# A decoder trunk on one core: a beginning with direct fp32 products, and three of four gate blocks as split fp32r products

## The chip, the cores and the metric

The kernel runs on one core of a Trainium2 chip. The metric is the device time of one execution in microseconds. The engines have these short names in the profile: PE (TensorE, matrix products), PEld (its weight loads), DVE (VectorE), ACT (ScalarE), POOL (GpSimd) and SP (SyncE, which issues most of the loads). Every engine has a queue of its own and works through it in order; they wait for each other by semaphores.

## The reference

The input is 256 tokens of 1024 features in float32. Layer 0 mixes tokens by a recurrent block, layer 1 by sparse attention; each is followed by an MLP with squared ReLU. Before each part stands an RMS norm, after it a residual addition. The change lies in the recurrent block:

```python
def _rglru_mixer(h, w_in, conv_w, conv_b, w_a, b_a, w_x, b_x, lam, w_out):
    proj = h @ w_in
    y = jax.nn.gelu(proj[..., :D_RNN], approximate=True)
    xb = _causal_depthwise_conv(proj[..., D_RNN:], conv_w, conv_b)
    xr = xb.reshape(B, S, RG_BLOCKS, RG_BLOCK_W)            # 4 blocks of 256
    r = jax.nn.sigmoid(jnp.einsum('bsnc,ncd->bsnd', xr, w_a).reshape(B, S, D_RNN) + b_a)
    i = jax.nn.sigmoid(jnp.einsum('bsnc,ncd->bsnd', xr, w_x).reshape(B, S, D_RNN) + b_x)
    log_a = -RG_C * r * jax.nn.softplus(-lam)
    a = jnp.exp(log_a)
    u = jnp.sqrt(-jnp.expm1(2.0 * log_a)) * (i * xb)
    _, hs = lax.associative_scan(_lru_combine, (a, u), axis=1)
    return (hs * y) @ w_out
```

## The kernel before

Features lie on the 128 partitions, tokens in the free dimension: a chunk is 128 features of 256 tokens, and there are eight (k = 0 to 7). Weights come in pieces of 128 by 1024 floats (512 KB), each holding the eight 128 by 128 blocks that give one chunk of output.

**Split products.** A float32 product is made of three fp32r products: weights and inputs are each split into a high part (a copy cast to fp32r) and a low part (the difference), and `mm3` adds high times high, high times low and low times high in PSUM (lines 344 to 346 in the profile). A piece is loaded by SP into a ring of raw tiles, cast to `whi` by ACT or DVE, and its `wlo` is made by DVE (lines 360 and 353). Pieces named in `AWAY` go another way: POOL issues a load that casts on its way into `whi` (line 384), ACT or DVE writes the negative into `wlo` (lines 356 and 357), and POOL issues the same load again, which adds into `wlo` (line 399).

**Direct products.** Gate blocks that are not in `GSPLIT`, which are blocks 0 and 1, keep raw float32 weights in tiles `gw`, and TensorE multiplies them as float32 (line 787).

**The order of the work.** The recurrent section is a list of tasks, each with engines, an assumed duration, keys that it reads and writes, and a wished time. `Plan.emit` makes an order from these in Python, before the kernel is built, with a seed (`SEEDS`), and emits every task into its engine's queue in that order. Assumed durations and lags of loads thus set the order, not the time. The order of the pieces is `RG_ORDER`: c0 to c7 are the input products with the conv behind them, y0 to y7 those of the gelu branch, g0 to g3 the gate blocks. Ring slots are given out by position in this order.

**The beginning.** SP loads the input x in four parts and the first three pieces (`NFINE`) in two halves each, in the order of `FIRST` ("x0" is chunks 0 and 1, "10" the first half of piece 1). Meanwhile TensorE runs 18 products of zeros (`WARM`, line 653), and eight more after the second chunk of piece 0. For every chunk ACT makes the high part `hh` of x times the norm's weight and DVE the low part `hl` (lines 660 and 662); for every quarter of the first three pieces the high and low parts are made separately. The norm's row scale `rs` is applied only to the product (lines 748 and 823), so that products begin before it is known.

**Behind it.** `conv` scales a product, runs the four taps on DVE and splits the result `xb` for the blocks in `GSPLIT`; `gate` makes the two gates by tanh (line 790), then the decay `r` and `t` (lines 797 and 799), which need `sp` and `nsp`. Those come from a softplus of the parameter lambda, computed on tiles of 128 by 8 as a polynomial (lines 693 to 708). `scan` takes the square root and runs the recurrence on DVE chunk by chunk (line 818), `product` multiplies by the gelu branch and splits the result (lines 830, 831, 360, 353), and the output projection follows.

Of the kernel before, what the change touches and what calls it, by code (L numbers as in the profile page):

```python
# [41 lines left out]
RG_ORDER = [(x[0], int(x[1])) for x in "c0 c1 c2 c3 c4 c5 c6 c7 y0 g0 g1 g2 y1 g3 y2 y3 y4 y5 y6 y7".split()]  # L42
# [11 lines left out]
GSPLIT = (2, 3)  # L54
AWAY = [("in", 1), ("in", 2), ("in", 4), ("in", 6)]
# [171 lines left out]
def trunk_kernel(ctx: ExitStack, tc: tile.TileContext, x_in, vec_in, const_in, w2_in, wts, out):  # L227
# [139 lines left out]
    class Section:  # L367
# [21 lines left out]
        def split(self, i, t, lead):  # L389
            t -= lead + AHEAD * away[i]  # L390
            self.load(i, t)
            n = piece_cols(order[i][0])
            hi, lo, rw = hi_t[i % NSPL], lo_t[i % NSPL], raw_of(i)
            rk = raw_key(i)
            if away[i] and i >= self.seen["split"]:
                hk, lk = ("hi", i % NSPL), ("lo", i % NSPL)
                self.add([("act", 0.95, 0.0), ("dve", 0.63, HPEN)], minus(lo[:, :n], hi[:, :n].bitcast(F32)), r=[hk], w=[lk], t=t)
                self.add("sp", ADD[0], lambda e: None, r=[hk], w=[("slot", -i), lk], t=t, lag=0.0)
                self.add("pool", ADD[1], lambda e: e.dma_start(lo[:, :n], source(i), accum_op=OP.add), r=[("slot", -i)], w=[lk], t=t, lag=ADD[2])
                self.seen["split"] = self.seen["lo"] = i + 1  # L400
            if i >= self.seen["split"]:
# [33 lines left out]
        def proj(self, name, idx, b, t, step, xs=None, xk=None, wide=False):  # L435
            wh, wl, wk = self.weight(name, idx, t)
            z = self.bank((name, idx), b, (lambda x: x) if wide else zcols)
            xs, xk = xs or [(hhw[:, k], hlw[:, k]) for k in range(KC)], xk or hkey
            for i in range(0, 4, self.join):
# [9 lines left out]
                self.add("pe", 0.68 * self.join, run, r=wk + list(xk[ks.start:ks.stop]), w=[("ps", b)], t=t + i * step)  # L449
# [161 lines left out]
    with ExitStack() as ph:  # L611
# [12 lines left out]
        def first_x(k):  # L624
            a, b = KC * (k > 0) + k * S, KC + (k + 2) * S
            src = x_in[P * a:P * b].rearrange("(p n) -> p n", p=P)
            first_load(xgt[:, a:b], src, [("xt", k), ("xt", k + 1)] + ["vec0"] * (k == 0), 0.66, 3.6 if k else 2.0)

        def first_w(i, q):
            o = offs[i] + P * q * 256  # L630
            src = wts[o:o + P * 512].rearrange("(p n) -> p n", p=P)
            first_load(raw_t[i][:, q * 256:q * 256 + 512], src, [("raw0", i, q), ("raw0", i, q + 1)], 0.66, 3.6 if q or i else 2.1)
        sec.plan.busy.update(pool=0.5, act=0.4, pe=4.4)
# [22 lines left out]
        x2 = rg.tile([P, KC, S], F32, name="x2")  # L656
        for k in range(KC):
            g = gm0[:, k:k + 1]
            t = 0.6 * k - 3
            add("act", 0.4, lambda e, k=k, g=g: e.activation(hh[:, k], xt[:, k], AF.Identity, scale=g),  # L660
# [28 lines left out]
        NT = 9  # L689
        cj = [1.0 / (2 * j + 1) for j in range(NT + 1)]  # L690
        V = ["vec"]
        small = lambda fn, r=(), w=(), eng="pool", t=8.0: add(eng, 0.45 if eng == "pool" else 0.1, fn, r=list(r), w=list(w), t=t)
# [4 lines left out]
        small(lambda e: e.tensor_scalar(s8, e8, 2.0, None, op0=OP.add), ["e8"], ["s8"], "dve")  # L697
# [4 lines left out]
        for j in range(NT - 1, 0, -1):  # L702
            small(lambda e, j=j: e.scalar_tensor_tensor(ac, ac, cj[j], s2, op0=OP.add, op1=OP.mult), ["s2"], ["ac"], "dve")
        small(lambda e: e.scalar_tensor_tensor(ac, ac, cj[0], s8, op0=OP.add, op1=OP.mult), ["s8"], ["ac"], "dve")
        small(lambda e: e.tensor_scalar(ac, ac, 2.0, None, op0=OP.mult), [], ["ac"])
        small(lambda e: e.tensor_tensor(sp, ac, nsp, op=OP.add), ["ac", "nsp"], ["sp"])
# [23 lines left out]
        def conv(m, t):  # L730
            b = nextbank()
            if m < NFINE:
                wh, wl, _ = sec.weight("in", 8 + m, t)
                z, zk = sec.bank(("in", 8 + m), b, zcols), ("ps", b)
                for k in range(KC):
                    def run(e, k=k):
                        w = slice(k * P, (k + 1) * P)
                        mm3(z(), wh[:, w], wl[:, w], hhw[:, k], hlw[:, k], k == 0, k == KC - 1)
                        if m == 0 and k == 1:
                            keep_warm(8)  # L740
                    add("pe", 0.323 + 0.9 * (m == 0 and k == 1), run, r=[("hi0", m, k // 2), ("lo0", m, k // 2), ("hi", m), ("lo", m), hkey[k]],
# [12 lines left out]
            if m // 2 not in GSPLIT:  # L754
# [12 lines left out]
        def gate(b, t):  # L767
# [27 lines left out]
            for m in ms:  # L795
# [10 lines left out]
                r=keys("r", m), w=keys("i", m), t=t + 3)  # L806

        def scan(m, t):
# [4 lines left out]
            for m in ms:  # L813
                if m % 2 == 0:
                    ip, tp = pair(i_b, m), pair(t_b, m)
                    add("dve", 0.6, lambda e, ip=ip, tp=tp: e.tensor_tensor(ip, ip, tp, op=OP.mult), r=keys("t", m),
                        w=keys("i", m), t=t)
                add("dve", 0.59, lambda e, m=m: e.tensor_tensor_scan(t_t[m], r_t[m], i_t[m], 0.0, op0=OP.mult, op1=OP.add),
                    r=[("r", m), ("i", m)], w=[("t", m)], t=t + 0.5)
# [852 lines left out]
```

## Time and profile before

| | |
|---|---|
| median of 3 runs | 549.14 us (549.08 to 549.91) |
| profiled execution | 548.89 us, of which the span 547.1 us |
| PE busy | 539.4 us, 99% of the span |
| PEld busy | 502.8 us |
| DVE busy | 444.2 us, 81% |
| ACT busy | 363.9 us, 67% |
| POOL busy | 28.0 us, 5% |
| TensorE clock granted, mean | 0.998 |
| loads and stores | 105.63 MB, mean 193 GB/s |

A row of a timeline gives the start, the duration (the first start to the last end where several alike are merged), the engine, the line, the operation with its output and inputs, and how often; in brackets stands the idle time before it and what ended that. A row of a group ends with the busy time in us, the mean in ns and the idle time before. The shares of busy time are means over stages with different limits, so the recurrent section, about the first 70 us, is read by itself.

### The profile page before, as it was taken

Reading aid. Unit: us, or ns where it says so; the run is one execution under the profiler, and the core shown is the slowest. Engines: PE = TensorE matmul, PEld = TensorE weight load, DVE = VectorE, ACT = ScalarE, POOL = GpSimd, SP = SyncE. Lnnn points to the kernel's source line nnn. Section 1 sums busy time; section 2 is a strip of 40 time slices with the busy share of each in tenths; the row PEclk is TensorE's granted clock in tenths of the full one; section 3 lists DMA queues with packets and bytes.
Section 4 is the critical chain, followed back from the end, with each engine's and each line's share of the span. In section 5 each row is a group of like instructions: output and inputs, shape, how many; then the busy total and the mean of one; then the engine's idle time right before and its main releaser. Section 6 shows DMA issues by size and latency. Waiting matters only on the chain.

```text
span 547.1 us, 10280 instructions
## 1 busy us (share of the span) xinstructions
PE 539.4 (99%) x3766; PEld 502.8 (92%) x3766; DVE 444.2 (81%) x969; ACT 363.9 (67%) x739; POOL 28.0 (5%) x50
## 2 busy tenths in 40 slices
PE   9999999999999999999999999999999999999995
PEld 9999999999998889999999999999999998888895
DVE  7999999797777456898939999989797778977945
ACT  7799666697877334346747999966787876433422
POOL 1131000000000000173000000000000000000000
PEclk9999999999999999999999999999999999999999
DMA  8977665486667764458765431353487666765502
GB/s 317 403 199 234 186 220 183 166 281 209 211 198 230 244 211 148 160 168 265 258 193 189 133 112 55 122 192 104 169 262 202 199 213 206 262 209 180 153 0 78
DMA packets 34690, 105.63 MB, mean 193 GB/s; under 512 B 3920, under 2 KB 9296, under 8 KB 34640
## 3 DMA queue, kind: packets, MB, share of 16 engines
q1 hardware_dynamic: 32432, 100.26, 56.1%
q0 software_dynamic: 1152, 4.19, 3.3%
q8 instruction: 30, 0.49, 0.4%
q10 hardware_dynamic: 1056, 0.52, 0.3%
q14 instruction: 20, 0.16, 0.1%
HBM read 101.32 MB, written 1.05 MB: 187 GB/s over the span
## 4 chain that ended last, share of the span: by engine, by line
PE 85%; DVE 8%; DMA 3%; ACT 2%; issue 1%; DVEq 0%; ACTq 0%; SPq 0%
PE bank L349 24%; PE bank L350 12%; PE bank L604 8%; PE bank L605 8%; PE bank L603 8%; PE bank L346 5%; PE bank L344 5%; PE bank L345 5%; PE bank L1332 3%; DVE wlo L353 2%; DMA raw<-in_dram 2%; PE bank L1313 2%; DVE xb L752 2%; PE bank L1259 1%; PE bank L1260 1%; PE bank L1166 1%
## 5 line engine op out<-in xcount | busy, mean ns | idle before, releaser
L349 PE MATMUL bank<-hhl,whi 128*128 128x512 f32 x512 | 167.9, 382 | 0.0
L288 ACT CAST whi<-raw 128x1024 fp32r<-128x1024 f32 x116 | 121.0, 1049 | 60.4 <-PE bank L605 57.8
L297 DVE TENSOR_TENSOR wlo<-raw,whi 128x1024 fp32r<-128x1024 f32 x115 | 141.9, 1236 | 23.3 <-ACT whi L288 22.8
L350 PE MATMUL bank<-hhl,wlo 128*128 128x256 f32 x512 | 139.6, 273 | 0.0
L349 PEld LDWEIGHTS bank<-hhl,whi 128*128 128x128 f32 x512 | 96.9, 189 | 13.4
L350 PEld LDWEIGHTS bank<-hhl,wlo 128*128 128x128 f32 x512 | 98.5, 192 | 0.0
L353 DVE TENSOR_TENSOR wlo<-raw,whi 128x1024 fp32r<-128x1024 f32 (+2 forms) x70 | 74.4, 1088 | 2.5 <-ACT whi L360 2.5
L603 PE MATMUL bank<-whi,uhl 128*128 128x512 f32 (+1 forms) x206 | 75.3, 366 | 0.0
L605 PE MATMUL bank<-whi,uhl 128*128 128x512 f32 (+1 forms) x206 | 75.2, 365 | 0.0
L604 PE MATMUL bank<-wlo,uhl 128*128 128x512 f32 (+1 forms) x206 | 75.2, 365 | 0.0
L344 PE MATMUL bank<-hhl,whi 128*128 128x256 f32 x256 | 70.7, 276 | 0.2 <-DVE tt L1090 0.2
L346 PE MATMUL bank<-hhl,wlo 128*128 128x256 f32 x256 | 70.6, 276 | 0.0
L345 PE MATMUL bank<-hhl,whi 128*128 128x256 f32 x256 | 70.5, 275 | 0.0
L360 ACT CAST whi<-raw 128x1024 fp32r<-128x1024 f32 (+2 forms) x60 | 58.8, 998 | 11.5 <-PE bank L345 6.1
L879 DVE CUSTOM_DVE_ANT_0 t<-bank,s 128x256 f32<-128x256 f32 x64 | 27.1, 423 | 34.4 <-ACT s L877 34.2
L344 PEld LDWEIGHTS bank<-hhl,whi 128*128 128x128 f32 x256 | 49.2, 192 | 0.2 <-PE bank L1120 0.2
L346 PEld LDWEIGHTS bank<-hhl,wlo 128*128 128x128 f32 x256 | 49.2, 192 | 0.0
L345 PEld LDWEIGHTS bank<-hhl,whi 128*128 128x128 f32 x256 | 49.2, 192 | 0.0
L603 PEld LDWEIGHTS bank<-whi,uhl 128*128 128x128 f32 x206 | 39.1, 190 | 4.7
L605 PEld LDWEIGHTS bank<-whi,uhl 128*128 128x128 f32 x206 | 39.1, 190 | 4.7
L604 PEld LDWEIGHTS bank<-wlo,uhl 128*128 128x128 f32 x206 | 39.1, 190 | 4.7
L877 ACT COPY s<-bank 128x256 f32<-128x256 f32 x64 | 23.6, 368 | 23.7 <-PE bank L350 23.7
(251 smaller groups left out, 1016.2 us busy)
## 6 DMA issues: line engine op xcount, KB each, us to landing
raw<-in_dram SPq DMA_DIRECT2D x169, 512.0 KB, 4.3
raw<-in_dram SPq DMA_DIRECT2D x4, 560.0 KB, 5.2
whi<-in_dram POOLq DMA_DIRECT2D x4, 512.0 KB, 6.6
wlo<-in_dram POOLq DMA_DIRECT2D x4, 512.0 KB, 6.3
raw<-in_dram SPq DMA_DIRECT2D x6, 256.0 KB, 4.5
y<-in_dram SPq DMA_DIRECT2D x2, 512.0 KB, 7.3
gw<-in_dram SPq DMA_DIRECT2D x2, 512.0 KB, 9.2
pT<-in_dram SPq DMA_DIRECT2D x2, 512.0 KB, 5.8
```

Source lines behind the costliest of these rows:

```text
L288: (act.copy if eng is None else eng.tensor_copy)(hi_t[i % NSPL][:, :n], raw_of(i)[:, :n])
L297: (eng or dve).tensor_tensor(lo[:, :n], raw_of(i)[:, :n], hi[:, :n].bitcast(F32), op=OP.subtract)
L344: pe.matmul(ps, wh, xh, start=start, stop=False)
L345: pe.matmul(ps, wh, xl, start=False, stop=False)
L346: pe.matmul(ps, wl, xh, start=False, stop=stop)
L349: pe.matmul(ps.rearrange("p (h a i) -> p h a i", h=2, i=2), wh, xhl, start=start, stop=False)
L350: pe.matmul(pairs(ps[:, S:]), wl, xhl[:, 0], start=False, stop=stop)
L353: return lambda e: e.tensor_tensor(o, a, h.bitcast(F32), op=OP.subtract)
L360: return lambda e: (e.copy if e is act else e.tensor_copy)(o, a)
L603: pe.matmul(z, uh, wh, start=first, stop=False)
L604: pe.matmul(z, uh, wl, start=False, stop=False)
L605: pe.matmul(z, ul, wh, start=False, stop=last)
```

## The change

- **Beginning.** For the first two chunks (`NX`) of the first three pieces TensorE multiplies raw weights by `xg`, which is x times the norm's weight in float32: six direct products in place of six split ones. The first quarters of these pieces are not split any more. `hh` and `hl` of the two chunks are still made, for later pieces, at a later wished time. Warm-up products go from 18 to 14, and the eight inside are gone.
- **Gate block 1** joins `GSPLIT`: its weights become a piece of the ring, its products split ones, and its `xb` is split. **Gate block 3** joins `AWAY`, so that its weights are split by the two loads.
- `xb` is split for two chunks at once. Piece 3 is split in two halves.
- **Softplus.** Seven terms instead of nine; each step is two small POOL instructions instead of one of DVE.
- **Scan.** One instruction for two chunks; POOL sets the first column of `r` of the second chunk to zero, so that nothing is carried over.
- In the order of pieces y1 moves ahead of g1 and g2, and y2 ahead of g3; the seed, the lags of the first loads and some assumed durations differ.

```diff
-SEEDS, ROUNDS, SHIFT = (15, 186), 6, 1.5
+SEEDS, ROUNDS, SHIFT = (12, 186), 6, 1.5
-WARM = 18
-NI, NFINE = 3, 3
+WARM = 14
+NI, NFINE, NX = 3, 3, 2
-RG_ORDER = "c0 c1 c2 c3 c4 c5 c6 c7 y0 g0 g1 g2 y1 g3 y2 y3 y4 y5 y6 y7"
+RG_ORDER = "c0 c1 c2 c3 c4 c5 c6 c7 y0 g0 y1 g1 g2 y2 g3 y3 y4 y5 y6 y7"
-GSPLIT = (2, 3)
-AWAY = [("in", 1), ("in", 2), ("in", 4), ("in", 6)]
+GSPLIT = (1, 2, 3)
+AWAY = [("in", 1), ("in", 2), ("in", 4), ("in", 6), ("gate", 3)]
...
+            if i == NFINE and i >= self.seen["split"]:
+                for h in range(2):
+                    w, hk, lk = slice(512 * h, 512 * h + 512), ("hi", i) + (1,) * h, ("lo", i) + (1,) * h
+                    self.add([("act", 0.53, 0.0), ("dve", 0.34, HPEN)], copy(hi[:, w], rw[:, w]), r=[rk], w=[hk], t=t + h)
+                    self.add("dve", 0.6, diff(lo[:, w], rw[:, w], hi[:, w]), r=[rk, hk], w=[lk], t=t + h)
...
+            if k < NX:
+                add([("dve", 0.2, 0.0), ("act", 0.4, 0.1)], lambda e, k=k, g=g: (
+                    e.activation(xg[:, k], xt[:, k], AF.Identity, scale=g) if e is act else
+                    e.tensor_scalar(xg[:, k], xt[:, k], g, None, op0=OP.mult)), r=[("xt", k), "vec0"], w=[("xg", k)], t=t - 3)
+                t = 3.0 + 0.6 * k
...
         for q in range(4):
             for i in range(NFINE):
+                if q < NX // 2:
+                    continue
...
-        NT = 9
+        NT = 7
-            small(lambda e, j=j: e.scalar_tensor_tensor(ac, ac, cj[j], s2, op0=OP.add, op1=OP.mult), ["s2"], ["ac"], "dve")
+            small(lambda e, j=j: e.tensor_scalar(ac, ac, cj[j], None, op0=OP.add), [], ["ac"])
+            small(lambda e: e.tensor_tensor(ac, ac, s2, op=OP.mult), ["s2"], ["ac"])
...
-                        mm3(z(), wh[:, w], wl[:, w], hhw[:, k], hlw[:, k], k == 0, k == KC - 1)
-                        if m == 0 and k == 1:
-                            keep_warm(8)
+                        if k < NX:
+                            e.matmul(pairs(z()), raw_t[m][:, w], walk(xg[:, k]), start=k == 0, stop=False)
+                        else:
+                            mm3(z(), wh[:, w], wl[:, w], hhw[:, k], hlw[:, k], False, k == KC - 1)
...
-            add(HI, copy(xbh_b[:, m], xb[m]), r=[bk], w=[("xbh", m)], t=t + 1)
-            add("dve", 0.34, diff(xbl_b[:, m], xb[m], xbh_b[:, m]), r=[bk, ("xbh", m)], w=[("xbl", m)], t=t + 1.3)
+            b2, h2, l2 = (pair(x, m) for x in (xb_b, xbh_b, xbl_b))
+            add(HI2, copy(h2, b2), r=keys("xb", m), w=keys("xbh", m), t=t + 1)
+            add("dve", 0.6, diff(l2, b2, h2), r=keys("xb", m) + keys("xbh", m), w=keys("xbl", m), t=t + 1.3)
...
+            add("pool", 0.06, lambda e: e.memset(r_t[m + 1][:, :1], 0.0), w=[("r", m + 1)], t=t + 3.5)
...
-                add("dve", 0.59, lambda e, m=m: e.tensor_tensor_scan(t_t[m], r_t[m], i_t[m], 0.0, op0=OP.mult, op1=OP.add),
-                    r=[("r", m), ("i", m)], w=[("t", m)], t=t + 0.5)
+                ts_, rs_, is_ = (pair(x, m).rearrange("p k s -> p (k s)") for x in (t_b, r_b, i_b))
+                add("dve", 1.1, lambda e, o=ts_, a=rs_, b=is_: e.tensor_tensor_scan(o, a, b, 0.0, op0=OP.mult, op1=OP.add),
+                    r=keys("r", m) + keys("i", m), w=keys("t", m), t=t + 0.5)
```

More of the change, by code (lines that the diff above doesn't have):

```diff
@@ L36 @@
 CST = (3.5, 7.5, 11.5, 15.2)
[L37 removed]
+SEEDS, ROUNDS, SHIFT = (12, 186), 6, 1.5
 HPEN, LPEN, APEN, LEAD = 0.5, 1.0, 0.0, 9.0
[L39 to L40 removed]
+WARM = 14
+NI, NFINE, NX = 3, 3, 2
 SQN = 2
[L42 removed]
+RG_ORDER = [(x[0], int(x[1])) for x in "c0 c1 c2 c3 c4 c5 c6 c7 y0 g0 y1 g1 g2 y2 g3 y3 y4 y5 y6 y7".split()]
 FIRST = "x0 00 10 x2 20 x4 02 12 x6 22 piece vec cst piece"
@@ L438, in proj @@
             xs, xk = xs or [(hhw[:, k], hlw[:, k]) for k in range(KC)], xk or hkey
+            wk = [wk] * 2 + [wk + [k + (1,) for k in wk] if piece_no[(name, idx)] == NFINE else wk] * 2
             for i in range(0, 4, self.join):
@@ L448, in run @@
                             mm3(z(), wh[:, w], wl[:, w], xs[k][0], xs[k][1], k == 0, k == KC - 1)
-                self.add("pe", 0.68 * self.join, run, r=wk + list(xk[ks.start:ks.stop]), w=[("ps", b)], t=t + i * step)
+                self.add("pe", 0.68 * self.join, run, r=wk[ks.stop // 2 - 1] + list(xk[ks.start:ks.stop]), w=[("ps", b)], t=t + i * step)
             return z, ("ps", b)
@@ L656, in trunk_kernel @@
         x2 = rg.tile([P, KC, S], F32, name="x2")
+        xg = rg.tile([P, NX, S], F32, name="xg")
         for k in range(KC):
@@ L696, in trunk_kernel @@
         small(lambda e: e.activation(e8, e8, AF.Exp, scale=-1.0), ["tab"], ["e8"], "act", 9.0)
-        small(lambda e: e.tensor_scalar(s8, e8, 2.0, None, op0=OP.add), ["e8"], ["s8"], "dve")
+        small(lambda e: e.tensor_scalar(s8, e8, 2.0, None, op0=OP.add), ["e8"], ["s8"])
         small(lambda e: e.reciprocal(s8, s8), [], ["s8"], "dve")
@@ L737, in run @@
                         w = slice(k * P, (k + 1) * P)
-                        mm3(z(), wh[:, w], wl[:, w], hhw[:, k], hlw[:, k], k == 0, k == KC - 1)
-                        if m == 0 and k == 1:
-                            keep_warm(8)
-                    add("pe", 0.323 + 0.9 * (m == 0 and k == 1), run, r=[("hi0", m, k // 2), ("lo0", m, k // 2), ("hi", m), ("lo", m), hkey[k]],
+                        if k < NX:
+                            e.matmul(pairs(z()), raw_t[m][:, w], walk(xg[:, k]), start=k == 0, stop=False)
+                        else:
+                            mm3(z(), wh[:, w], wl[:, w], hhw[:, k], hlw[:, k], False, k == KC - 1)
+                    rk = ([("raw0", m, k // 2), ("raw", m), ("xg", k)] if k < NX else
+                          [("hi0", m, k // 2), ("lo0", m, k // 2), ("hi", m), ("lo", m), hkey[k]])
+                    add("pe", ((0.86, 0.6)[k] if m == 0 else 0.43) if k < NX else 0.323, run, r=rk,
                         w=[zk], t=m * 0.33 + k * NI * PJ / 2 if m < NI else t + k * PJ / 2)
@@ L812, in scan @@
                 w=[("t", m) for m in ms], t=t)
[L813 to L818, printed above, removed]
-                    r=[("r", m), ("i", m)], w=[("t", m)], t=t + 0.5)
+            for m in range(m, m + SQN, 2):
+                ip, tp = pair(i_b, m), pair(t_b, m)
+                add("dve", 0.6, lambda e, ip=ip, tp=tp: e.tensor_tensor(ip, ip, tp, op=OP.mult), r=keys("t", m),
+                    w=keys("i", m), t=t)
+                ts_, rs_, is_ = (pair(x, m).rearrange("p k s -> p (k s)") for x in (t_b, r_b, i_b))
+                add("dve", 1.1, lambda e, o=ts_, a=rs_, b=is_: e.tensor_tensor_scan(o, a, b, 0.0, op0=OP.mult, op1=OP.add),
+                    r=keys("r", m) + keys("i", m), w=keys("t", m), t=t + 0.5)
         def branch(m, t):
```

14 lines of the change are left out of this document (7 added, 7 removed).

## The prediction

> **What bounds the kernel now.** I read the page first (busy time, then the chain that ended last), then the table of windows, the chain of waits inside the recurrent section, and the timeline of TensorE around each place that the change touches.
>
> ```profile
> span 547.1 us, 10280 instructions
> ...
> PE 539.4 (99%) x3766; PEld 502.8 (92%) x3766; DVE 444.2 (81%) x969; ACT 363.9 (67%) x739; POOL 28.0 (5%) x50
> ```
> ```profile
> 31.70:55.00 23.30, 23.30 (x182) 22.48 (x181) 22.85 (x46) 23.10 (x49) 4.39 (x8) 1.00 0.76 204
> 55.00:67.60 12.60, 12.47 (x111) 12.19 (x109) 12.60 (x20) 8.14 (x11) 0.00 (x0) 1.00 0.61 173
> 67.60:250.00 182.40, 182.40 (x1125) 168.05 (x1126) 140.95 (x210) 114.43 (x202) 14.05 (x13) 1.00 0.63 203
> ```
>
> Columns of the window rows: length, then PE, PEld, DVE, ACT and POOL busy. TensorE is occupied nearly always, so a time saved on it counts if the others follow. From 67.6 us on they do: DVE has 41 us spare before 250. In the recurrent section they barely do: from 31.7 to 55.0 TensorE, DVE (22.85 of 23.30) and ACT (23.10) are full together, and from 55.0 to 67.6 DVE is. The last waits of TensorE there are short:
>
> ```profile
> 63.58 0.28 PE L345 MATMUL bank<-xbl,whi 128*128 128x256 f32 x1
> 63.75 0.38 PE L346 MATMUL bank<-xbh,wlo 128*128 128x256 f32 x1
> ...
> 67.17 0.28 PE L345 MATMUL bank<-xbl,whi 128*128 128x256 f32 x1
> 67.57 0.38 PE L346 MATMUL bank<-xbh,wlo 128*128 128x256 f32 x1
> ...
> 68.23 0.32 PE L345 MATMUL bank<-xbl,whi 128*128 128x256 f32 x1
> 68.39 0.28 PE L346 MATMUL bank<-xbh,wlo 128*128 128x256 f32 x1
> ```
>
> Starts normally follow each other by 0.11 us. The longest gap, 67.17 to 67.57, is 0.29 us too long; with five smaller ones from the first (63.58) to the last (68.23) it is 0.68 in all. So TensorE's work sets the end, with DVE and ACT less than a microsecond behind. Everything the change does lies before 68 us; the saving there passes one for one to the end. The sums are made against the profiled execution: 548.89 us, 1.79 above its span and 0.25 below the median of 549.14.
>
> **The start.** The relevant rows of TensorE and of ACT:
>
> ```profile
> 3.49 0.91 ACT L660 ACTIVATE hhl<-xt 128x256 fp32r<-128x256 f32 x2 [1.25 <-DMA xt<-in_dram]
> 4.30 0.39 ACT L360 CAST whi<-raw 128x256 fp32r<-128x256 f32 x1
> 5.29 0.27 PE L344 MATMUL bank<-hhl,whi 128*128 128x256 f32 x1
> 5.40 0.28 PE L345 MATMUL bank<-hhl,whi 128*128 128x256 f32 x1
> 6.05 1.11 PE L653 MATMUL bank<-warm 128*128 128x256 f32 x8
> 6.95 0.41 ACT L360 CAST whi<-raw 128x256 fp32r<-128x256 f32 x1 [0.21 <-DMA raw<-in_dram]
> 7.00 0.27 PE L344 MATMUL bank<-hhl,whi 128*128 128x256 f32 x1
> ```
> ```profile
> 4.43 0.84 PE L653 MATMUL bank<-warm 128*128 128x256 f32 x3
> 4.86 0.59 PE L653 MATMUL bank<-warm 128*128 128x256 f32 x2
> ```
>
> Before: 18 warm-up products to 5.29, two chunks of piece 0, eight more warm-ups (6.05 to 7.00), then a stream without a gap. A split product is three passes of 0.11, so 0.333 us. The six products of pieces 0 to 2 with chunks 0 and 1 are paid for by 7.00 + 4 x 0.333 = 8.33.
>
> A direct fp32 product is priced by the gate blocks, the nearest row:
>
> ```profile
> 31.77 6.21 PE L787 MATMUL bank<-xb,gw 128*128 128x256 f32 x28
> ...
> 37.92 0.28 PE L345 MATMUL bank<-xbl,whi 128*128 128x256 f32 x1
> ```
>
> The 28 records are 14 products, two records each; with the switch back to fp32r they take 37.92 - 0.11 - 31.77 = 6.04 us: 0.43 each, 0.10 more than a split product. After the change four warm-ups are gone, so the place of the 15th, 4.43, is the first direct product's. Its operands are there: xg is one DVE scaling of x, which landed before 3.49, and piece 0 landed before 4.30. The warm-ups at 4.43 and 4.86 are two steps of 0.21 apart, the products from 5.29 on stand 0.11 apart at the same width: the array ran at half speed until about 5.3. So the first direct product costs 0.86 (to 5.29), three more 0.43 each (to 6.6), and the two of piece 2 wait for its load, which reached ACT at 6.95: 6.93 + 0.87 = 7.80. Gain: 8.33 - 7.80 = **0.53**. That load, not the clock, fixes it. Ends: 0 (later chunks catch up on DVE and nothing is kept) and 0.9 (chunk 2 fills the wait: 4.43 + 0.43 + 6 x 0.43 = 7.44).
>
> [...]
>
> **What must keep up there.** Skipped are three splits of 256 columns; two scalings by DVE are new; piece 3 (conv chunk 3) is split in halves.
>
> ```profile
> L353 DVE TENSOR_TENSOR wlo<-raw,whi 128x256 fp32r<-128x256 f32 x12 | 4.6, 422 | 0.0
> ...
> L360 DVE CAST whi<-raw 128x256 fp32r<-128x256 f32 x7 | 1.9, 290 | 0.0
> ```
> ```profile
> 11.64 1.06 ACT L360 CAST whi<-raw 128x1024 fp32r<-128x1024 f32 x1 [0.18 <-DMA raw<-in_dram]
> ...
> 23.40 1.09 DVE L748 TENSOR_TENSOR xp<-bank,rstd 128x256 f32<-128x256 f32 x3 [0.41 <-ACT rstd L465]
> ```
>
> DVE loses 3 x 0.42 + 3 x 0.29 and gains 2 x 0.29: 1.5 us less before 23.4, so it can feed a TensorE that is 0.5 earlier. Piece 3 lands at 11.6 and is wanted at 7.80 + 18 x 0.333 = 13.8; its first half needs half a cast (0.53) and half a subtraction (about 0.6): 12.8. Without the halves it would be 11.64 + 1.06 + 1.2 = 13.9, just late; so they cost nothing and cover the advance. The sums of squares and the row scale (23.40) stand behind the same DVE work and can come 0.5 (with TensorE) to 1.5 us (with DVE) sooner; I take 0.9, near the middle, since ACT's casts of arriving weights stand between.
>
> **Gate block 1** goes from direct fp32 to split: eight products at 0.43 become eight at 0.333: **0.79** less on TensorE; ends 0.6 and 0.9 (the switch between the kinds is in the 0.43 and may stay). The other engines pay:
>
> ```profile
> 31.93 0.07 DVE sp L703
> ...
> 35.56 1.14 DVE wlo L353
> 36.70 0.34 DVE xbl L353
> ...
> 63.69 0.63 DVE xbl L353
> ```
> ```profile
> 54.45 2.43 DVE L818 TENSOR_TENSOR_SCAN t<-r,i 128x256 f32<-128x256 f32 x4
> 56.80 0.67 DVE L816 TENSOR_TENSOR i<-i,t 128x512 f32<-128x512 f32 x1
> ```
> ```profile
> L360 ACT CAST xbh<-xb 128x256 fp32r<-128x256 f32 x3 | 1.2, 395 | 0.1
> ```
>
> DVE after 23.4: block 1's weights +1.14, its activations as a pair +0.63; gate 3's weights leave DVE, -1.14 (a DMA adds instead; the negation that takes the cast's place on ACT or DVE is as long as that cast); blocks 2 and 3 in pairs, 2 x 0.63 for 4 x 0.34, -0.10; scans, eight at (56.80 - 54.45)/4 = 0.59 become four of twice the length, an estimate of 1.1 each, -0.3; the polynomial, eight steps at 0.07 and a small add and a final one moved or fused, -0.7. Net **-0.5**. ACT: +1.06 for block 1's cast and two 0.39 less what pairing saves, about +0.6. ACT has 8.40 - 7.06 us idle before 31.7 (row below), where the cast can go, as piece 10 needs the slot of piece 3 only, free at about 16.5; so 0.6 falls into the full stage, as much as DVE loses there.
>
> ```profile
> 23.30:31.70 8.40, 8.40 (x78) 8.40 (x77) 8.30 (x27) 7.06 (x12) 2.93 (x6) 1.00 0.96 335
> ```
>
> So TensorE comes to its waits at 63 to 68 us by 0.53 + 0.79 = 1.32 sooner and DVE's products by 0.9 + 0.5 = 1.4: the 0.68 of waits stays, **0**. Ends: -0.68 (all waits gone) and +1.1 (neither the earlier row scale nor the 0.5 is kept because ACT is full).
>
> **Moves without a price of their own.** The polynomial goes to POOL: seven terms, twelve steps there instead of eight on DVE, and a few more.
>
> ```profile
> 11.94 0.91 POOL L695 TENSOR_SCALAR hb<-vec 128x16 f32<-128x16 f32 x1 [10.61 <-DMA vec<-in_dram]
> ...
> 33.41 0.39 POOL L705 TENSOR_SCALAR sp<-sp 128x8 f32<-128x8 f32 x1 [2.74 <-DVE sp L704]
> 33.89 0.20 POOL L706 TENSOR_TENSOR sp<-sp,sp 128x8 f32<-128x8 f32 x1
> 34.18 0.35 POOL L707 TENSOR_SCALAR sp<-sp 128x8 f32<-128x8 f32 x1
> ```
> ```profile
> 36.69 0.60 ACT L797 ACTIVATE t<-r,sp 128x256 f32<-128x256 f32 x1
> ```
>
> A step pair is 34.18 - 33.41 = 0.77. From the exponential at about 23.4: four steps and the reciprocal 2.2, six pairs 4.6, the end 1.6, two or three DMA issues between them 2: 33.6, ahead of ACT's first use at 36.69. The cover is 3.1 us over about 17 steps. POOL also gets block resets of r for the joined scans; they wait for DVE's gate products, and behind them on its queue stand only loads for y pieces. Gate 1's load of 512 KB only moves on SP's queue, from a tile of its own to the ring of pieces. Gate 3 leaves that queue; POOL issues two loads for it instead, beside the four pairs it has:
>
> ```profile
> whi<-in_dram POOLq DMA_DIRECT2D x4, 512.0 KB, 6.6
> ```
>
> Its slot comes free with conv piece 6, about 25; 25 + 6.6 + 1.1 for the negation + about 1 for queueing + as long again for the adding load: 40.4, wanted near 44. Half a megabyte more crosses a DMA that is 0.76 busy there. If that cover went, TensorE would wait for gate 3 or run y pieces first. Order and seed of the planned queue change too; they have no row, and lie inside the ends of the waits.
>
> **Sum.** -0.53 - 0.79 + 0 = -1.3: 548.89 - 1.3 = 547.6 for such an execution, 547.8 beside the median.
>
> **Rivals.**
> 1. ACT and DVE bind (same). From 31.7 to 55 ACT is 23.10 of 23.30 and gets 0.6; if the row scale comes only 0.5 sooner and ACT's 0.6 isn't covered, DVE's products come 0.5 sooner and the waits grow by 0.8: -0.5, 548.6. For it: those rows. Against: ACT's idle before 31.7 and after 55 (8.14 of 12.60).
> 2. Full relief (faster). DVE keeps all 1.5 + 0.5 us; the 0.68 of waits goes: -2.0, 547.1. Against: no row says that the waits would go before new ones come.
> 3. POOL is late (slower). It decides in one place, ACT's first tanh with sp: the cover of 3.1 over 17 steps is used up when a step takes 0.18 more than 0.38, that is 0.56, and the forecast's gain when it takes 0.64. The row at 11.94 has 0.91: 17 x 0.53 - 3.1 = 5.9 late, ACT in order, 553.7 if nothing is caught up. Against: the rows at 33 to 34 us, while DVE was busy throughout. [...]
> [...]
>
> **How the numbers follow.** A difference of 0.2%, 1.1 us, is about what a measurement can tell from no change. Chances: forecast 0.50 (0.9 to 1.7 us gained, four fifths of it beyond 1.1), full relief 0.16, ACT and DVE bind 0.20, late clock 0.04, late POOL or another queue 0.10. Faster 0.40 + 0.16 = 0.56; same 0.10 + 0.20 + 0.04 = 0.34; slower 0.10. The range goes from a little beyond full relief, 546.7, to the late clock, 549.1.
>
> **What would show it.** Direct products from about 4.4 us, the first at half rate, the last of the six done near 7.8, no eight warm-ups after; a dense stream to the gates; 16 records instead of 32 of direct gate products; the row scale near 22.5; the last POOL step before ACT's first tanh with sp; waits of TensorE between 60 and 68 of 0.7 or less; from there to the end the same distances as before, 1.3 us sooner. It is wrong if TensorE waits for xbl or wlo by more than 1.5 us before 68, or ACT waits for sp.

## The result and the profile after

The changed kernel is slower: 552.8 us at the median of eight runs (550.88 to 553.25) against 549.08 us (548.63 to 549.91, eight runs on the same chip), ratio 1.0051 with an interval of 1.0035 to 1.0067 (the two medians alone are 0.68% apart; what follows goes by the ratios, each to the kernel before on the same chip). Forecast were 547.8 us and a range up to 549.1. The eight times fall into two groups, three at 550.9 to 551.0 and five at 552.8 to 553.3; the profiled execution, 552.77 us with a span of 551.0, is of the second.

The head of the page of the kernel after: TensorE is busy 1.6 us longer than before although it has less to do.

```profile
span 551.0 us, 10254 instructions
...
PE 541.0 (98%) x3756; PEld 502.5 (91%) x3756; DVE 443.6 (81%) x955; ACT 364.7 (66%) x738; POOL 40.1 (7%) x67
```

Nearly all of it lies before the MLP. The first product of 512 columns, a marker behind everything that the change touches, starts at 84.92 us before and at 88.70 after: 3.78 of the 3.9 us by which the spans differ.

```profile
84.92 0.38 PE L349 MATMUL bank<-hhl,whi 128*128 128x512 f32 x1
```
```profile
88.70 0.38 PE L349 MATMUL bank<-hhl,whi 128*128 128x512 f32 x1
```

**The beginning after** (timeline of TensorE, start and duration): twelve records of direct products from 4.44, two to a product, then split products from 8.85. The first split record starts right behind the last direct one (8.82), which still takes its 0.27 us, and the second comes 0.35 later instead of 0.11; so the split products count from 9.09, where before they were at 8.33. In these two profiles that is 0.76 later, against a forecast of 0.53 sooner.

```profile
4.44 4.82 PE L754 MATMUL bank<-xg,raw 128*128 128x256 f32 x12
8.85 0.52 PE L344 MATMUL bank<-hhl,whi 128*128 128x256 f32 x1
```

**The gate blocks after.** All that is left of direct gate products is block 0, sixteen records instead of 32, 0.22 us apart as before: by count and price the 0.79 us are there.

```profile
L806 PE MATMUL bank<-xb,gw x16: 379/379/382, 31.4 to 35.3; 128*128 128x256 f32 x16
```

**At 60 us** TensorE stops for 2.46 us, from 60.62 to 63.08, for the low part of y6, whose adding load POOL had issued at 55.91. The chain that ended last, cut to these microseconds, begins with that load, 7.12 us under way:

```profile
60.62 0.28 PE L345 MATMUL bank<-hhl,whi 128*128 128x256 f32 x1
...
63.08 0.38 PE L346 MATMUL bank<-hhl,wlo 128*128 128x256 f32 x1 [2.18 <-DMA wlo<-in_dram]
```
```profile
55.91 7.12 DMA wlo<-in_dram
63.03 0.04 issue
63.08 0.38 PE bank L346
```

And 1.3 us after the pause the array runs at half clock for 3.4 us (windows; the number 0.50 is the granted clock): 18 records where 33 would stand (the count of the same stretch in experiment 2, at 1.00), about 1.7 us lost.

```profile
64.40:67.80 3.40, 3.40 (x18) 3.40 (x17) 3.40 (x6) 3.37 (x5) 0.00 (x0) 0.50 0.39 112
```

So +0.76 - 0.79 + 2.35 (the pause less one regular step) + 1.7 = 4.0, against the 3.8 measured.

**Why the load is late** is read backwards. POOL's queue after (the bracket is the idle time before and what ended it): in front of the load stands the fourth reset of r, which waits 5.92 us for DVE's gate product.

```profile
49.39 0.10 POOL L826 MEMSET r<- 128x1 f32 x1 [1.23 <-DVE i L824]
55.41 0.10 POOL L826 MEMSET r<- 128x1 f32 x1 [5.92 <-DVE i L824]
55.91 0.85 POOL L399 DMA_DIRECT2D wlo<-in_dram  x1 [0.40 <-issue]
```

DVE in turn had stood for a raw piece, with the negation of y6 (L357) behind it, which the load needs too:

```profile
51.38 0.69 DVE L360 CAST whi<-raw 128x1024 fp32r<-128x1024 f32 x1 [2.05 <-DMA raw<-in_dram]
51.99 1.22 DVE L353 TENSOR_TENSOR wlo<-raw,whi 128x1024 fp32r<-128x1024 f32 x1
53.13 0.69 DVE L357 TENSOR_SCALAR wlo<-whi 128x1024 fp32r<-128x1024 f32 x1
```

And SP's queue shows why the raw pieces came late. Before, three of them were issued at 23; after, one is issued at 17.79 and nothing more until 39.58.

```profile
23.06 1.29 SPq L274 DMA_DIRECT2D raw<-in_dram  x3
```
```profile
17.79 1.44 SPq L274 DMA_DIRECT2D raw<-in_dram  x1
39.58 0.87 SPq L274 DMA_DIRECT2D raw<-in_dram  x2
```

The reason is arithmetic. A ring slot belongs to a position in the order of pieces, (i - 7) modulo 5 behind the first seven. In the changed order y5 is piece 16 and gate 2 piece 11, both in slot 4, and gate 2 is split only at about 39.5. Before they were pieces 15 and 9, in slots 3 and 2, and slot 3 was free early. SP issues in order, so y5's load stops that of y7 too; the output pieces behind them leave at 43.7, as before (44.2). All then cross between 40 and 60 us, together with POOL's. Before (first fence) that stretch began with an idle DMA (columns at the end: clock, DMA share, GB/s); after (second) it is full throughout:

```profile
40.00:45.00 5.00, 5.00 (x46) 4.98 (x45) 5.00 (x9) 5.00 (x14) 0.55 (x1) 1.00 0.28 85
45.00:50.00 5.00, 5.00 (x47) 5.00 (x47) 4.55 (x8) 4.98 (x12) 0.88 (x1) 1.00 0.92 284
```
```profile
40.00:45.00 5.00, 4.99 (x43) 4.72 (x42) 4.97 (x10) 4.73 (x11) 0.64 (x2) 1.00 1.03 226
45.00:50.00 5.00, 5.00 (x47) 5.00 (x46) 4.33 (x7) 4.19 (x8) 1.50 (x4) 1.00 1.05 397
```

A third oddity stands at the start of POOL's queue: one operation on 128 by 8 numbers that took 8.05 us, and a load for y1 behind it, issued at 21.48 (before, the first such load left at 17.43).

```profile
13.48 8.05 POOL L709 TENSOR_SCALAR sp<-vec 128x8 f32<-128x8 f32 x1
21.48 0.77 POOL L384 DMA_DIRECT2D whi<-in_dram  x1
```

The theories for the tests: **the slot** (y5 behind gate 2) as the root; as rivals **the resets** on POOL, **the block** of 8 us on POOL, and a loss in **the beginning**. Below, "plan unchanged" means that every engine has its instructions in the order of the changed kernel, but for the edit.

### The profile page after: what moved, and what is told of

It reads as the page before. It is cut to its first block, busy times and chain, and to the rows that moved or that the text cites. A ratio compares the mean times of both kernels' runs of the same rounds, so it can differ in the third digit from the quotient of the medians.

```text
span 551.0 us, 10254 instructions
## 1 busy us (share of the span) xinstructions
PE 541.0 (98%) x3756; PEld 502.5 (91%) x3756; DVE 443.6 (81%) x955; ACT 364.7 (66%) x738; POOL 40.1 (7%) x67
## 3 DMA queue, kind: packets, MB, share of 16 engines
HBM read 101.85 MB, written 1.05 MB: 187 GB/s over the span
## 4 chain that ended last, share of the span: by engine, by line
PE 86%; DMA 1%; DVE 1%; ACT 0%; issue 0%; DVEq 0%; ACTq 0%
PE bank L349 24%; PE bank L350 12%; PE bank L612 8%; PE bank L610 8%; PE bank L611 8%; PE bank L344 6%; PE bank L346 6%; PE bank L345 6%; PE bank L1352 3%; PE bank L1333 2%; DMA wlo<-in_dram 1%; PE bank L1279 1%; PE bank L1280 1%; PE bank L1186 1%; PE bank L1187 1%; PE bank L1188 1%
## 5 line engine op out<-in xcount | busy, mean ns | idle before, releaser
L353 DVE TENSOR_TENSOR wlo<-raw,whi 128x1024 fp32r<-128x1024 f32 (+3 forms) x68 | 73.3, 1102 | 2.6 <-ACT whi L360 2.5
L344 PE MATMUL bank<-hhl,whi 128*128 128x256 f32 x250 | 69.8, 279 | 0.2 <-DVE tt L1110 0.2
L345 PE MATMUL bank<-hhl,whi 128*128 128x256 f32 x250 | 69.3, 277 | 0.0
L360 ACT CAST whi<-raw 128x1024 fp32r<-128x1024 f32 (+3 forms) x59 | 58.1, 1002 | 13.8 <-PE bank L345 8.1
```

The costliest lines, as they stand in the source:

```text
L344: pe.matmul(ps, wh, xh, start=start, stop=False)
L345: pe.matmul(ps, wh, xl, start=False, stop=False)
L353: return lambda e: e.tensor_tensor(o, a, h.bitcast(F32), op=OP.subtract)
L360: return lambda e: (e.copy if e is act else e.tensor_copy)(o, a)
```

## The experiments

**1. The resets on DVE.** Plan unchanged; the four resets are issued by DVE.

```diff
-add("pool", 0.06, lambda e: e.memset(r_t[m + 1][:, :1], 0.0), ...)
+add("pool", 0.06, lambda e: dve.memset(r_t[m + 1][:, :1], 0.0), ...)
```

> The changed kernel with one thing moved: the four resets of r for the joined scans are issued to DVE instead of POOL, at the same places of the planned order; all other queues are the same. Theory Q (POOL's queue): the fourth reset waits for DVE's last gate product (55.27 us) and stands ahead of the adding load of piece y6, which therefore is issued at 55.91 though its negated weights are ready at 53.8; it lands 7.1 us later, at 63.08, and TensorE waits 2.35 us from 60.73; 1.3 us later the clock halves for 3.4 us, which costs 1.7. So here: issue at about 54, landing at about 61.1, a wait of 0.4, no half clock; 552.8 - 2.0 - 1.7 = 549.1. Theory D (the transfers are full from 40 to 55 us, so the load is late whenever it is issued): landing again near 63, 552.8. If the wait goes but the clock halves all the same: 550.8.

Measured: 551.46 us (550.51 to 552.43), ratio 1.0043 [1.0030, 1.0056]. Neither expectation is met: the load is issued at 54.96, 0.95 sooner but not at 54, since now it waits for DVE's negation, which is late as well; TensorE still waits, though no half clock follows in this profile (64.4 to 67.8 at 1.00):

```profile
62.15 0.38 PE L346 MATMUL bank<-hhl,wlo 128*128 128x256 f32 x1 [1.50 <-DMA wlo<-in_dram]
```

By itself the reset would be some 0.4 us of the loss, by the two ratios, but their intervals overlap.

**2. The pause filled.** Eighteen products of zeros ahead of y6's first low-part product, so that TensorE works while it waits.

> The changed kernel with 18 products of zeros (18 x 0.11 = 2.0 us) put into TensorE's queue just ahead of the product of y6 that waits for its low part; nothing else is changed, so the wait for the load stays (landing at about 63.1), but TensorE is busy during it. Theory C (the halved clock from 64.4 to 67.8 comes from TensorE's pause): no half clock, 1.7 us less than the changed kernel, 551.0, and one group of times instead of two (550.9 and 553.0). Rival (the clock halves for another reason, say by the phase of some period): still 552.8 with two groups.

Measured: 551.77 us (551.29 to 553.12), ratio 1.0055 [1.0041, 1.0069]. In the profiled execution (551.29 us) the low-part product comes at 63.28, as late as in the changed kernel, and the half clock is gone:

```profile
64.40:67.80 3.40, 3.40 (x33) 3.40 (x32) 3.40 (x6) 3.29 (x5) 0.00 (x0) 1.00 0.31 95
```

So the half clock follows the pause. It also makes up the two groups of times: in the changed kernel the mean granted clock is 0.997 in the three runs of 550.9 to 551.0 and 0.994 or 0.995 in the five of 552.8 to 553.3, and none of the five runs here is below 0.996. But the ratio isn't lower than the changed kernel's, against the expected 551.0: the wait stays, the beginning was late here (split products from 9.08), and one run with a clock of 0.996 took 553.12. What that run lost stays open.

**3. Eighteen warm-ups again**, on top of experiment 1 (`WARM = 18`).

> As e1_reset_on_dve, with 18 warm-up products instead of 14: the first direct product goes on at about 5.3 us instead of 4.44. Theory L (the loads of pieces 1 and 2 and of chunk 2 set the start): the six direct products end where they end in the changed kernel (about 9.1) or sooner, since more of them run at full clock, and the time is that of e1 within 0.3. Rival (the earlier first product counts): 0.85 more than e1.

Measured: 550.74 us (550.47 to 552.22), ratio 1.0036 [1.0023, 1.0048]. The direct products start at 5.15 instead of 4.44, and split products begin at 8.46, in the versions with 14 warm-ups at 8.13 to 9.08. The time is that of experiment 1 within the intervals, so the warm-ups aren't what the result lacks.

**4. The kernel before once more**, one profiled run beside these.

> The kernel before, unchanged, for a second profile of its start. If the late landing of the first loads in the profile of the changed kernel (chunk 2 reached ACT at 7.12 against 5.82) is chance of a run, starts differ by as much here; if it belongs to the changed kernel, chunk 2 is there at 5.8 again and the dense stream begins at 7.0. Time 549.1.

It took 551.51 us. The start does differ by chance: the second part of x reached ACT at 6.74 instead of 5.82. And its profile shows the same wait at y6. DVE stood for a raw piece ahead of the negation, as in the changed kernel though without its slot conflict; y6's adding load left at 54.22 (in the first profile at 52.42) and took 9.25 us to land (DVE, then TensorE):

```profile
51.44 0.70 DVE L360 CAST whi<-raw 128x1024 fp32r<-128x1024 f32 x1 [1.66 <-DMA raw<-in_dram]
```
```profile
63.52 0.38 PE L346 MATMUL bank<-hhl,wlo 128*128 128x256 f32 x1 [2.32 <-DMA wlo<-in_dram]
```

The kernel before stands near the same edge and fell over it in one of its two profiles; the changed kernel fell over it in its only one.

**5. y5 in another slot.** Plan unchanged; y5's load goes to slot 0, which is free early.

```diff
 def raw_of(i):
+    if order[i] == ("in", 5):
+        return raw_t[0]
```

> The changed kernel with one thing different: the raw weights of piece y5 are loaded into raw tile 0 instead of raw tile 4. All queues keep their order. Theory R (ring): as gate block 1 became a piece and the order moved, y5 shares its raw tile with g2, whose split is done at 39.4 us; SP's queue stands from 17.8 to 39.58 us behind that load, so y5, y7 and the first out pieces are loaded between 39.6 and 51 instead of at 23, the transfers are full from 40 to 58, DVE waits 2.05 us for raw weights at 51.4, negates y6 late, and the adding load of y6 lands at 63.1. Here y5 goes out at about 18 to 21 and y7 by 26, DVE's wait for raw weights at 51 goes, the negation comes 2 us sooner; the wait of TensorE at 60.6 falls from 2.35 to 0.5 or less and the half clock goes: 552.8 - 2.0 - 1.7 = 549.1. Rival A (the doubled load of gate 3 fills the transfers): wait 1.5 or more, 551 to 553.

Measured: 550.7 us (548.87 to 553.64, 12 runs), ratio 1.0023 [1.0008, 1.0038]: by the ratios more than half of the loss is gone, though less than expected (549.1). TensorE's wait falls from 2.18 to 0.97, where 0.5 or less was expected, and no half clock follows in this profile (64.4 to 67.8 at 1.00). SP's loads follow each other again from 17 to 23 us (first row, in the profile of this version), DVE's wait for a raw piece is gone, y6's load leaves at 54.08, now held by the reset (second fence, POOL):

```profile
17.45 6.07 SPq L276 DMA_DIRECT2D raw<-in_dram  x3
```
```profile
53.58 0.10 POOL L828 MEMSET r<- 128x1 f32 x1 [3.36 <-DVE i L826]
54.08 0.85 POOL L401 DMA_DIRECT2D wlo<-in_dram  x1 [0.40 <-issue]
```

**6. Slot and resets together.** Edits 1 and 5.

> e4 and e1 together: y5 in raw tile 0 and the resets of r on DVE. If after e4 the reset still holds the adding load of y6 on POOL (in the changed kernel from 53.8 to 55.9), this is 0.3 to 1.0 below e4, at about 548.3; if e4 leaves no wait, it equals e4 within 0.3.

Measured: 549.81 us (548.63 to 551.04, 12 runs), ratio 1.0006 [0.9995, 1.0017]: no difference from before that the interval can tell, and 0.9 us below experiment 5, as expected. The load leaves at 52.15 and in the profile TensorE doesn't wait for y6 at all. Resets alone (experiment 1) against both is the clearest price of the slot: 1.0043 to 1.0006, 2.0 us, with intervals apart.

**7. Gate block 1 back to direct products**, with a new plan (`GSPLIT = (2, 3)`).

> The changed kernel with gate block 1 direct again (its weights in a tile of their own), everything else as changed; the order is planned anew. Theory R: in this order y5 falls on the raw tile of g2 again (pieces 15 and 10, five apart), so SP's queue stands still again and the wait at y6 stays: 551 or more, plus 0.79 for the direct products. Rival B (the extra split of block 1 on DVE and ACT makes DVE late): the wait goes, 549.1 + 0.3 = 549.4 or less.

Measured: 555.9 us (554.59 to 557.14), ratio 1.0123 [1.0106, 1.0141]. y5's load does stand behind gate 2 here too, though gate 1 is out of the ring; gate 2's split ends at 36.06 and the load leaves (SP's queue):

```profile
36.14 0.33 SPq L274 DMA_DIRECT2D raw<-in_dram  x1
```

But the expected wait at y6 isn't there: in this plan its load leaves at 50.62, and the longest wait of TensorE is for activations (2.2 us for xbh). So a shared slot costs only what the plan behind it makes of it.

**8. The beginning of before with y5 in another slot**, with a new plan (`NX = 0`, 18 and 8 warm-ups, the old lags).

> e4 with the beginning of before: 18 warm-up products, eight more after the second chunk, the first two chunks as split products, lags of before; planned anew. Read from the profile: products done by 20 and 31 us. Theory S (loads landing set the beginning, 7 to 9 us, so direct products gain nothing): 38 to 39 products by 20 us as in the changed kernel (38) and in before (39 and 38), and a time within 0.5 of e4. Rival (the forecast's 0.53): 0.5 or more above e4.

Measured: 557.86 us (556.74 to 558.95), ratio 1.0151 [1.0134, 1.0168]. Neither 7 nor 8 says what its part is worth: the planner made another order from the changed list of tasks, with waits of its own (TensorE's, in the profile of 8):

```profile
PE bank L346 <- ACT xbh L362: 3.0, 1, 3.0
PE bank L348 <- DMA wlo<-in_dram: 2.1, 1, 2.1
PE bank L347 <- DVE xbl L355: 1.3, 1, 1.3
```

These orders stand 3 us above the changed kernel and 7 above experiment 5, which they were made from, several times the change's own terms. From here on the plan stayed as it was.

**9. y6's adding load cut** to 128 of 1,024 columns, in the changed kernel, plan unchanged.

```diff
-e.dma_start(lo[:, :n], source(i), accum_op=OP.add)
+e.dma_start(lo[:, :n], source(i)[:, :n], accum_op=OP.add)   # n = 128 for y6
```

> The changed kernel with the order of every engine as it is; only the adding load of y6 brings 128 of its 1,024 columns (64 KB in place of 512 KB), so the low part of seven eighths of that one weight piece is left without the original weights. It prices the wait for this transfer and the half clock behind it, with nothing else moved. Theory (slot conflict, late transfer): the load is issued at 55.9 as before but lands some 3 to 5 us sooner (before about 60), TensorE's wait of 2.46 at 60.6 and the half clock of 64.4 to 67.8 go, some of the short waits at 64 to 68 of the kernel before may come back (0.3 to 0.7): 552.8 - 2.4 - 1 to 1.7 + 0.5 = 549.2 to 550. Rival (the loss lies in the beginning and in waits spread over the section, and what is won at y6 is lost at the next wait): 551.5 or more.

Measured: 550.64 us (550.42 to 551.44), ratio 1.0031 [1.0019, 1.0043]; between the two expectations. It leaves at 55.22, lands in 3.5 us, TensorE doesn't wait for it and the clock stays full (64.4 to 67.8 at 1.00). But nearly half of what is won goes to the next waits, for the activations that ACT and DVE split late:

```profile
63.20 0.38 PE L344 MATMUL bank<-xbh,whi 128*128 128x256 f32 x1 [0.40 <-ACT xbh L360]
64.00 0.38 PE L345 MATMUL bank<-xbl,whi 128*128 128x256 f32 x1 [0.42 <-DVE xbl L353]
```

So the 4 us at y6 are 1 to 2 us of the result: 2.2 by the medians, 1.1 by the ratios, whose intervals overlap. That the next wait comes from DVE's standstill at 49 to 51 us fits the rows, and wasn't tried by itself.

**10. Slot, resets and 18 warm-ups.**

> The version with y5 in another slot and the resets on DVE, and 18 warm-up products in place of 14 at the start. If the beginning is set by the half clock that the first direct products run at (two records of 0.43 each in place of 0.21), four warm-ups more take 0.86 us of the half-rate time from them and cost their own time: the dense stream begins within 0.2 us of the 8.38 there, and the time is that of the version without them, 549 to 550, ratio to the kernel before 1.000 within 0.0015. If the forecast's step were right that the third load alone fixes it, also no change. A gain of 0.5 or more would say that the warm-ups that were taken out carried the clock.

Measured: 550.02 us (548.25 to 550.65, 12 runs), ratio 1.0009 [0.9999, 1.0020], as expected no change against experiment 6. Split products begin at 8.69, a little later than expected (within 0.2 of 8.38).

**11. Slot, resets, and POOL's blocked operation on DVE.**

```diff
-small(lambda e: e.tensor_scalar(nsp, lam, -1.0, 0.0, ...), V, ["nsp"])
+small(lambda e: dve.tensor_scalar(nsp, lam, -1.0, 0.0, ...), V, ["nsp"])
```

> The same version (y5 in another slot, resets on DVE), and POOL's one small operation on lambda (nsp, 128x8, which took 8.05 us in the changed kernel between 13.5 and 21.5, with POOL's queue behind it) given to DVE at its planned place, one instruction of about 0.1 us there. POOL's issue of y1's cast load should come near 17 in place of 21.5, and with it the loads that it issues after it. Theory: POOL's block is hidden, since the loads that decide (y6's add) are held by DVE's and SP's order: no change, 549 to 550, ratio 1.000 within 0.0015. Rival (the block delays the whole chain of POOL's loads): y6's add load is issued 1 us sooner than at 52.15 and the time falls by 0.5 to 1 us.

Measured: 548.41 us (548.07 to 549.19, 11 runs) against 549.2 of before on the same chip (548.42 to 552.43, 23 runs), ratio 0.9982 [0.9969, 0.9994]: the only version that beats both kernels, by an interval that just excludes no change, and less scattered than experiments 5, 6 and 10. My theory was wrong here: the block wasn't hidden. But the rival's place was wrong too, since y6's load leaves at 52.23, not sooner than in experiment 6. What went is the scatter: experiment 10, on the same chip and with four more warm-ups, has times from 548.25 to 550.65, and its profiled one (550.35 us) shows y1's load behind the block, at 21.03, and a wait that this version doesn't have:

```profile
36.70 0.38 PE L348 MATMUL bank<-xbh,wlo 128*128 128x256 f32 x1 [0.92 <-DVE wlo L355]
```

That this wait is what the block costs in the slower runs is a reading of one profile, not shown.

**12. That operation on DVE alone**, slot and resets as in the changed kernel.

> The changed kernel with POOL's one small operation on lambda given to DVE, and nothing else: y5 stays in the slot that it shares with gate 2, the resets of r stay on POOL. It tells which of the three side effects carries the loss. Theory (slot conflict first): y1's cast load is issued near 15 in place of 21.5, but SP still stands from about 17.8 to 39 behind y5's load, the transfers run full from 40 to 60, y6's adding load is issued near 55 to 56 and TensorE waits 2 us for it: 551.5 to 552.5, ratio 1.004 to 1.006. Rival (POOL's block is the root, since every later load of POOL starts from it): the load is issued before 53.5, the wait is under 1 us, 550 or less, ratio below 1.002.

Measured: 551.9 us (550.44 to 553.0), ratio 1.0044 [1.0029, 1.0059], as the first theory expected. y1's load leaves at 15.14, six microseconds sooner, and y6's at 55.69 all the same; the wait is there, and so is the half clock (second fence, clock 0.50):

```profile
62.98 0.38 PE L346 MATMUL bank<-hhl,wlo 128*128 128x256 f32 x1 [2.58 <-DMA wlo<-in_dram]
```
```profile
63.70:67.05 3.35, 3.35 (x18) 3.35 (x18) 3.35 (x5) 3.13 (x4) 0.00 (x0) 0.50 0.21 43
```

Together:

| version, plan unchanged | ratio to before | y6's load issued | TensorE's wait for it |
|---|---|---|---|
| changed kernel | 1.0051 [1.0035, 1.0067] | 55.91 | 2.18 |
| block on DVE (12) | 1.0044 [1.0029, 1.0059] | 55.69 | 2.58 |
| resets on DVE (1) | 1.0043 [1.0030, 1.0056] | 54.96 | 1.50 |
| resets, 18 warm-ups (3) | 1.0036 [1.0023, 1.0048] | 55.14 | 1.88 |
| slot (5) | 1.0023 [1.0008, 1.0038] | 54.08 | 0.97 |
| slot and resets (6) | 1.0006 [0.9995, 1.0017] | 52.15 | none |
| slot, resets, 18 warm-ups (10) | 1.0009 [0.9999, 1.0020] | 53.74 | 0.37 |
| slot, resets, block (11) | 0.9982 [0.9969, 0.9994] | 52.23 | none |

The slot is the largest. The others seem to count for more once it is mended, since the waits stand one behind the other: the resets 0.9 us instead of 0.4, the block 1.3 to 1.5 instead of 0.4. Of these steps only the last has intervals that are apart.

## Why the prediction was wrong

**The start, -0.53: wrong in size, and its sign isn't seen.** The last direct product is paid for at 8.62 in experiment 6 and 8.69 in experiment 11, counted as above, not at 7.80; before it was 8.33 in the first profile and 8.5 in the second, which short waits just behind bring to 8.6. Two terms of the sum were too small. The price of a direct product, 0.43 "by the gate blocks, the nearest row", doesn't hold here: at full clock the records stand 0.27 apart, 0.55 a product, in the gates 0.22. And "the array ran at half speed until about 5.3" was true of the execution before; in experiment 6 it lasts to about 7.0. There no load is waited for, and twelve records run one behind the other, six 0.43 apart (first row, starts 4.4 to 6.6) and six 0.27 (second, 7.0 to 8.3):

```profile
L756 PE MATMUL bank<-xg,raw x6: 578/627/629, 4.4 to 6.6; 128*128 128x256 f32 x6
L756 PE MATMUL bank<-xg,raw x6: 436/437/438, 7.0 to 8.3; 128*128 128x256 f32 x6
```

From 4.43 that makes 8.63. Why the price differs from the gates' stays open; the code reads `xg` by turns from its two halves (`walk`) and the gates' `xb` in order, and that this is the reason wasn't tried. So the step "That load, not the clock, fixes it" is wrong for these executions. In experiment 5 it is right, with another time than the 6.95 of before: the products of piece 2 wait for their load until 7.55, and four records later the split ones begin, at 8.50:

```profile
7.55 1.35 PE L756 MATMUL bank<-xg,raw 128*128 128x256 f32 x4 [0.19 <-DMA raw<-in_dram]
8.50 0.52 PE L346 MATMUL bank<-hhl,whi 128*128 128x256 f32 x1
```

The loads of the first microseconds scatter by about a microsecond between executions (ACT got the second part of x at 5.82 and 6.74 in the two profiles of before, at 5.79 to 7.12 in the ten with the changed plan), and I read one execution as the rule. Further on, the 25th product of these pieces starts at 14.37 and 14.66 in the two profiles of before and at 14.40 to 15.35 in those ten: no gain is seen, and the first profile of before, from which the sum was made, was a lucky one.

**Gate block 1, -0.79: right** by the count and the price of the records; no run tells it apart, since the plan of experiment 7 was another. The marker of experiment 11 stands at 84.76 and that of before at 84.92, of experiment 6 at 84.62:

```profile
84.76 0.38 PE L351 MATMUL bank<-hhl,whi 128*128 128x512 f32 x1
```

+0.36 for the start and -0.79 for the gate make -0.43 for experiment 11; -0.16 is seen, and the other 0.3 isn't accounted for. With its side effects mended the change is worth 0.16 to 0.30 us on profiles without the wait at y6, at most a quarter of the 1.3. The median of experiment 11 is lower by 0.8, its lowest time by 0.35 (548.07 against 548.42); that the rest is the executions in which before meets y6's wait, as in experiment 4, fits the ranges of the times but wasn't counted.

**DVE 0.9 to 1.4 ahead: not seen.** The row scale was to come near 22.5; the first product is scaled at 23.4 (first start in this group of the kernel after), as before. TensorE's start, which it was to follow, hadn't come sooner.

```profile
L766 DVE TENSOR_TENSOR xp<-bank,rstd x5: 373/414/425, 23.4 to 28.1; 128x256 f32<-128x256 f32 x5
```

**The waits at 63 to 68 "stay", 0, ends -0.68 and +1.1: wrong, by a mechanism that I didn't price.** Two steps failed, both moves that I put at nothing. The first is "Order and seed of the planned queue change too; they have no row, and lie inside the ends of the waits." Before, gate 2 and y5 stood six pieces apart; with y1 moved ahead of gate 2 they stand five apart, and five is the number of slots. That gate 1's load "only moves on SP's queue, from a tile of its own to the ring of pieces" isn't the cause of this meeting: it moves both by one, and in experiment 7, without it, they meet as well. (By the same arithmetic gate 1 in the ring with the old order would have put y3 behind gate 1; that wasn't run.) The slot of y5 is worth 1.5 us alone (1.0051 to 1.0023, intervals just overlapping) and 2.0 on top of the resets (1.0043 to 1.0006). The second step is that of the resets, of which I wrote that "behind them on its queue stand only loads for y pieces": just such a load is what TensorE waited for. Together with the slot that is 0.45% (1.0051 to 1.0006), in two parts of which the resets are the smaller. I named what stands behind the waiting instruction and didn't ask how late it may come. Before, y6's load left at 52.42 and nothing waited; a profile of the same kernel in which it left at 54.22 and took 9.25 us to land waits 2.3 us. And the loads that cross at the same time met a DMA share of 1.03 to 1.05 from 40 to 50 us, where I had counted on "a DMA that is 0.76 busy there", its mean from 31.7 to 55.0 before.

**The full cover of the polynomial: right where I looked.** (Its terms add to 33.8, not 33.6; nothing hangs on that.) Its last step ended at about 36.7 and ACT's first tanh with sp began at 37.01, so rival 3 isn't the cause.

```profile
36.43 0.31 POOL L723 TENSOR_SCALAR sp<-sp 128x8 f32<-128x8 f32 x1
```

But the price per step from rows at 33 us, 0.20 to 0.39, doesn't hold ahead of them: at 13.48 one operation took 8.05 us, while DVE ran subtractions and sums without a gap until 21.5. In the profile of experiment 6 DVE stops at 19.35 for 1.36 us (last row), and there the operation ends, after 6.91:

```profile
12.55 6.91 POOL L711 TENSOR_SCALAR sp<-vec 128x8 f32<-128x8 f32 x1
...
19.41 0.76 POOL L386 DMA_DIRECT2D whi<-in_dram  x1
```
```profile
20.71 1.23 DVE L355 TENSOR_TENSOR wlo<-raw,whi 128x1024 fp32r<-128x1024 f32 x1 [1.36 <-ACT whi L362]
```

In both profiles the operation ends where DVE's run of instructions of two inputs first breaks, at about 21.5 and 19.4. But a run of them isn't enough to hold POOL so long: before, the same operation took 1.25 us while DVE went on without a gap from 11.6 to 18.4.

```profile
12.82 1.25 POOL L694 TENSOR_SCALAR sp<-vec 128x8 f32<-128x8 f32 x1
```

What made it 8 us in the one kernel and 1.25 in the other wasn't tried.

**Gate 3 by DMA: hidden as forecast**; no wait of TensorE for it stands out in the profile after, though its two loads are among those that fill the DMA. **The late clock**, with 0.04 among the chances and 549.1 as the end of the range, is a full clock so late that the forecast's gain is lost, a term that no run shows. What the runs showed: half speed lasts to about 7.0 in experiments 6 and 11, against the 5.3 of the forecast, and the last direct product is paid for at 8.62 and 8.69, 0.82 and 0.89 behind the 7.80, of which the price of 0.55 is a part. Half clock cost another 1.7 us where the forecast hadn't looked, behind the pause at 60 us. The forecast's own sign of being wrong, a wait for wlo of more than 1.5 us before 68, is what happened.

## What to carry to other kernels

A piece added to a ring changes the slot of every piece behind it, and a piece moved in its order changes which pieces meet in one: write down, for each later load, which earlier use its slot now waits for, and remember that a wait on the issuing queue is passed on to all loads behind it (here from 17.79 to 39.58 us on SP's). For every instruction put ahead of a DMA issue on a queue, work out when that transfer must leave to land in time, and compare that with the latest of several executions, not with one. Take the price of an instruction from rows of the same operands and clock, and look at the start in several executions. If a hand-made plan is made anew, a part can't be judged by taking it back alone: keep the order and change one thing in it.

## What the runs showed of the hardware

- A pause of 2.46 us on TensorE (the changed kernel) was followed, 1.3 us after work had resumed, by 3.4 us at half clock (64.41 to 67.82 at 0.50); a pause of 2.86 us (experiment 12) after 0.7 us and one of 2.15 us (experiment 3, row below) after 0.5 us by as much. After a pause of 2.60 us in experiment 4 no half clock came (64.4 to 68.0 at 1.00), nor after 1.77 us in experiment 1 (64.4 to 67.8 at 1.00) or 1.25 us in experiment 5 (the same), and none when the pause was filled. So the length of the pause alone doesn't decide in these profiles: after 2.15 us it came, after 2.60 it didn't. What else does wasn't shown.

```profile
63.00:66.40 3.40, 3.40 (x18) 3.40 (x18) 3.40 (x7) 2.45 (x4) 0.00 (x0) 0.50 0.01 2
```

- A POOL operation on 128 by 8 numbers, of a kind that takes 0.2 to 0.4 us elsewhere, lasted 8.05 and 6.91 us beside a run of DVE instructions of two inputs, and held POOL's DMA issues with it, to 21.48 and 19.41; in the kernel before it lasted 1.25 us beside such a run (11.6 to 18.4).
- A direct fp32 product of 128 by 256 took 0.43 us at full clock in the gates and 0.55 in the beginning (experiment 6, records 0.27 apart); a split one of three fp32r passes takes 0.333. A switch between the kinds costs nothing that the rows show: the next pass starts 0.35 us after the first, which is the last direct record's 0.27 and a pass's 0.11, less 0.03.
- A load of 512 KB that adds took 7.12 us to land at 56 us and 9.25 in the profile of before in experiment 4; the cut one of 64 KB took 3.5.
